# A hybrid SSD and attention layer on one core: the first head pair's softmax scaling as one GpSimd product per tile, and one weight remainder on GpSimd

## The chip, the core and the metric

The kernel runs as one program on one core of a Trainium2 chip. The core's engines are called by short names here: PE multiplies matrices (PEld is its weight load), DVE, ACT and POOL (GpSimd) are the three engines for elementwise work, and SP only issues DMAs. The metric is the device time of one execution in microseconds (us); lower is better. Each engine works through its own instructions strictly in the order in which they were issued to it, so an instruction that waits holds up everything behind it on its engine.

## The reference

One layer is computed for 512 frames of a new stream and 64 frames of a running one (256 past frames), 576 tokens in all. What matters here is the attention half, an MLA with 8 heads, and the end of the SSD half:

```
y   = y_scan + d_skip * xh
y   = y.reshape(T, 512) * silu(z)
y_ssd = rmsnorm(y, ssd_norm)                      # gate and norm of the SSD half

s   = (q_lat @ keys_c.T + q_rope @ keys_r.T) * scale
s   = where(causal, s, -inf)
w   = softmax(s)                                  # exp(s - max) / sum, per row and head
o   = (w @ keys_c) @ w_uv                         # per head

x   = x + concat([y_ssd, o]) @ w_out
x   = x + (silu(hf @ w_gate) * (hf @ w_up)) @ w_down,  hf = rmsnorm(x)
```

## The kernel before, in words

Activations lie with channels on the 128 partitions and the 576 tokens along the free axis. A product in near full precision is made of three passes: each weight tile and each operand is split into a high part (rounded on ACT) and a low part, the remainder (on DVE, one subtraction); `split_weights` (lines 107 to 113) does it for weights. The remainders of the weights of the four head pairs are called `wl_pair`, those of the output product `wl_out`.

The heads are handled in four pairs p = 0 to 3. `pair_proj(p)` (L610) loads and splits a pair's weights, and issues four DMAs on POOL's queue (L616) that copy the rotary rows of the queries into `qs`, of which there are two buffers, used by turns. `scores(p, i)` (L665) makes the score products of a query tile i: tiles 0 to 3 hold 128 new-stream queries each and see 128, 256, 384 or 512 keys per head; tile 4 holds the running stream's 64 queries of both heads, stacked on the partitions, and sees 320 keys. `soft` (L648) then does the softmax: per head a row maximum on DVE (L655) and an exponential on ACT (L656) that also sums each row into `sm`, one reciprocal of the sums on DVE (L657), and the scaling of each head's probabilities `pr` by its inverse sum, head 0 on DVE (L662) and head 1 on ACT (L660). `turn` and `turn_s` (L684, L698) transpose the probabilities on PE (`ptp`) for the value product.

Between these stand the steps of the SSD half's end. `norm_y` makes the factor `Ry` in two halves of 288 tokens: L173 `nr_v` and L178 `nr_u` and L179 `Ry` on DVE, three activations on ACT. `cat_tile(t)` scales one of four channel tiles by `Ry` on DVE (L764, `xsd`), rounds it on ACT (L143) and takes the remainder on DVE (L145, both parts are called `cat_y`). `out_tile` for F0 is the first product that uses `cat_y` (PE, `ps_o`, L458); its sums are added to x on DVE (L750).

The order of the program's steps is written by hand as strings of step names:

```
ORDER_ATT = "q11 N S03 y0 y1 y2 S01 S02 S00 S04 S13 y3 T00 X t0 S12 S11 T02 T01 F0 S14 p2 q20 V0 k20 k21 q21 S23 ..."
```

S03 is `scores(0, 3)`, N `norm_y`, y0 to y3 `cat_tile`, T and t the transposes, F0 the first output tile, p2 and p3 `pair_proj`. The order in which each engine issues its instructions is then fixed by a second set of tables, one list of places per engine (`ISSUE`), in which pieces of later steps go ahead of earlier ones; `issue_in_order` ties each instruction of an engine to the one before it.

Of the kernel before, what the change touches and what calls it, by code (L numbers as in the profile page):

```python
# [1350 lines left out]
173 189 182 184 190-191 179 192-194 185-186 220 195 204-206 196-202 207 282 208 212-214 209 216 218 215 210 221 217 219  # L1351
222-225 228 226-227 229-230 239 249 240 231 288 250 241 233 242 251 253 252 254 234 232 258 235 255 236 257 256 301 261
237 259 238 260 243 262 264 245 263 247 244 268 246 248 269-270 283 265 284 271-273 289 280 274 276 275 281 266 291 311
285 277 312 267 292 296 293 310 294 278-279 313 297 300 286-287 290 303 306 298 320 299 304 302 307 321 356 305 322 316
295 317 308 357 324 318 314 323 309 330 315 319 358 327 361 331 325-326 359 334 332 328-329 335 338 343 333 344 339 336
340 346 345 337 349 352 360 341 353 351 342 354 350 347 355 362 371 348 364-365 363 366 369-370 367-368 376 384 372 378
377 379-380 373 383 381 374 391 382 375 387 399 389 385 390 388 386 394 393 395 392 397 396 414 400 398 402 401 403 406
404 411 408 405 407 412 456 410 415 417 413 458 419 416 418 409 427 425 420 426 423 422 421 432 424 428 463 457 430 429
431 433 436 435 437 460 434 438 445 459 440 461-462 446-447 439 441 449 448 442 467 469 450 471 470 468 451 466 464 472
452-453 443-444 473 454 475 474 455 465 476 485 481 477 490-491 478 482 492-493 483 494-496 479-480 497 504 484 509-512  # L1360
516 486 498 513 500 514 501 515 502 526-529 533 540 487-489 530 541-543 499 505-506 503 517 531 523-524 518-519 507-508
525 532 534 522 544 535 560 520 536 521 545 537 539 546 538 561-562 547-548 563 549 568 564 550-553 555 569-570 554 559
571 556 572-575 565 576-577 566 557 584-585 578 586 579-580 558 592 567 593-594 587-588 581-582 595 583 597 596 589
598-601 590 604 591 602-603 614-617 605 621 606 618 607-608 619-620 613 628-630 622 631 611 632 612 623 610 609 624 635
633 625 634 627 626 648-650 636 651 637 656 652 638-641 643 657-658 642 647 659 644 660-663 653 664-665 654 645 672-673
666 674 667-668 646 680 655 681-682 675-676 669-670 683 671 685 684 677 686-689 678 692 679 690-691 702-705 693 709 694
706 695-696 707-708 701 716-718 710 719 699 720 700 711 698 697 712 723 721 713 722 715 714 736-738 724 739 725 744 740
726-729 731 745-746 730 735 747 732 748-751 741 752-753 742 733 760-761 754 762 755-756 734 768 743 769-770 763-764
757-758 771 759 773 772 765 774-777 766 780 767 778-779 790-793 781 797 782 794 783-784 795-796 789 804-806 798 807 787
# [8 lines left out]
136 127 137 134 128 140 135 124 121 120 139 129 138 141 130 123 143 131 125 150 146 149 132 210 133 145 148 154 152 151  # L1378
147 158-159 157 144 155 160-162 153 164-165 212 170 172 171 166 168 180 186 169 181 174 187 175 173 176 189 167 190 177
227 178 192 179 193 188 182 195 194 191 183 200 196 184-185 199 201 197 213 208 215-216 202-203 219 209 204 217 234 218  # L1380
198 205-206 211 214 226 220 233 221 240 207 223 242 224 222 241 229 243-244 225 271 235 230 228 231 238 237 272 232 245
236 248 239 246 249-252 247 257 255 261 254 262 256 259 263 258 278 265 253 267 266 264 268-270 260 273-277 284 280-282
285 287 283 279 293 286 291 288 290 289 302 292 294 296 295 298 300 297 301 303-304 299 309 305-306 310 307 312 329 308
311 316-317 313-315 330 318 331 319-320 332 336 321-325 333 337 335 334 326 338 340 339 327 346 343 328 344 355-356
341-342 347-348 357 349 358 350 363 352 351 353 345 354 372 359 373 360-361 374-375 382-383 364-370 384 371 376 362 381
385 380 386 377 379 378 390-392 388 387 389 393 401 394 402 395 400 397 399 396 409 398 410 403 418-419 405-408 411 420
413 421 414-415 412 416-417 404 422 427 424 428 423 425-426 435-436 429 444-445 431-433 430 434 437 446 438 447 440-441
439 442-443 448 456-457 449 458 450 454 451 455 453 452 459 464 460 465-466 462 461 463 467 475 468 476 469 474 471 473
470 483 472 484 477 492-493 479-482 485 494 487 495 488-489 486 490-491 478 496 501 498 502 497 499-500 509-510 503
518-519 505-507 504 508 511 520 512 521 514-515 513 516-517 522 530-531 523 532 524 528 525 529 527 526 533 538 534  # L1390
539-540 536 535 537 541 549 542 550 543 548 545 547 544 557 546 558 551 566-567 553-556 559 568 561 569 562-563 560
564-565 552 570 575 572 576 571 573-574 583-584 577 592-593 579-581 578 582 585 594 586 595 588-589 587 590-591 596
604-605 597 606 598 602 599 603 601 600 607 612 608 613-614 610 609 611 615 623 616 624 617 622 619 621 618 632 620 633
625 641-642 628-631 634 643 636 644 637-638 635 639-640 626 645 650 627 651 647-648 646 649 659-660 652 668-669 655-657
653 658 661 670 663 671 664-665 662 666-667 672 677-678 654 679 675 673-674 676 680-682 684 683 685-687
# [110 lines left out]
```

## Time and profile before

| | before |
|---|---|
| time, median of 3 runs | 635.08 us (634.49 to 635.43) |
| the profiled execution's own time | 634.74 us |
| its span | 633.0 us |
| mean granted TensorE clock | 0.998 |
| busy: PE, DVE, ACT, POOL | 98%, 85%, 63%, 19% |

The span is the stretch from the first to the last instruction in the trace; the 1.7 us more of the execution's own time lie around it. Busy shares are those of the whole span. The place that the change touches is a stretch of some 20 us about a quarter of the way in, from 143 to 163 us, where the SSD half ends and the attention begins.

### The profile page before, as it was taken

What the parts mean: (1) busy time and instruction counts of PE and PEld (TensorE: products, weight loads), DVE (VectorE), ACT (ScalarE), POOL (GpSimd) and SP (SyncE); (2) the same over time, 40 slices, a digit from 0 to 9 for tenths busy, and PEclk for the clock granted to TensorE, in tenths of its full rate; (3) what the DMA queues carried; (4) which work ended last, traced back from release to release, by engine and by line L of the source; (5) the groups of instructions that cost most, each with busy time, mean ns of one, the idle gap of its engine ahead of it and who ended that gap; (6) DMA issues with size and microseconds to landing.
All of it is one profiled execution on the core that took longest, in us unless ns stands there. A gap on an engine that the chain in (4) does not pass through costs nothing.

```text
span 633.0 us, 12094 instructions
## 1 busy us (share of the span) xinstructions
PE 622.7 (98%) x4635; PEld 596.3 (94%) x4635; DVE 539.3 (85%) x939; ACT 400.4 (63%) x768; POOL 117.7 (19%) x170
## 2 busy tenths in 40 slices
PE   9999999999999999999999999999999999999995
PEld 9899999986787899999999999999999999999995
DVE  6999986789776699999999888988899789976555
ACT  7655346779775567666556676566657665767364
POOL 1322104231010000001301330033104220323323
PEclk9999999999999999999999999999999999999999
DMA  8322374413231223335743986397738893689924
GB/s 320 134 61 74 95 193 127 128 61 106 77 117 34 96 72 126 89 106 178 262 128 90 221 182 152 82 193 185 169 100 162 199 202 101 100 215 251 256 41 149
DMA packets 39593, 89.19 MB, mean 141 GB/s; under 512 B 4570, under 2 KB 14312, under 8 KB 39280
## 3 DMA queue, kind: packets, MB, share of 16 engines
q1 hardware_dynamic: 26416, 63.12, 31.0%
q0 software_dynamic: 12400, 24.73, 21.3%
q8 instruction: 36, 0.59, 0.4%
q10 hardware_dynamic: 720, 0.57, 0.3%
q14 instruction: 21, 0.17, 0.1%
HBM read 62.74 MB, written 24.53 MB: 138 GB/s over the span
## 4 chain that ended last, share of the span: by engine, by line
PE 88%; DVE 6%; ACT 2%; issue 2%; POOL 1%; DMA 1%; POOLq 0%; DVEq 0%
PE ps_x L874 21%; PE ps_d L1064 14%; PE ps_z L874 10%; PE ps_in L281 7%; PE ps_y L874 5%; PE ps_o L458 4%; PE ps_z L458 4%; PE ps_first L129 3%; PE ps_d L281 2%; PE sc L672 2%; PE ps_p L874 2%; PE ps_l L281 2%; PE pv L719 1%; PE ptp L694 1%; PE ps_q L458 1%
## 5 line engine op out<-in xcount | busy, mean ns | idle before, releaser
L874 PE MATMUL ps_x<-xop,wh_gu_S 128*128 128x288 f32 x378 | 76.9, 295 | 0.0
L112 DVE TENSOR_TENSOR wl_gu_S<-gu,wh_gu_S 128x1024 fp32r<-128x1024 f32 x44 | 53.3, 1220 | 9.1 <-ACT wh_gu_S L111 6.2
L874 PEld LDWEIGHTS ps_x<-xop,wh_gu_S 128*128 128x128 f32 x378 | 60.5, 188 | 0.0
L1078 POOL DMA_DIRECT2D acc<-fz x32 | 27.9, 902 | 166.5 <-ACT fz L1075 137.8
L111 ACT CAST wh_gu_S<-gu 128x1024 fp32r<-128x1024 f32 x44 | 46.3, 1053 | 16.3 <-PE ps_y L874 8.3
L874 PE MATMUL ps_x<-xop,wl_gu_S 128*128 128x288 f32 x189 | 55.8, 295 | 0.0
L281 PE MATMUL ps_in<-xs,wh_in 128*128 128x256 f32 (+1 forms) x256 | 51.2, 296 | 0.4 <-DVE sp_a L361 0.4
L281 PEld LDWEIGHTS ps_in<-xs,wh_in 128*128 128x128 f32 x256 | 40.8, 188 | 1.2 <-issue 1.1
L281 PE MATMUL ps_in<-xs,wl_in 128*128 128x320 f32 (+1 forms) x128 | 37.7, 295 | 0.0
L874 PEld LDWEIGHTS ps_x<-xop,wl_gu_S 128*128 128x128 f32 x189 | 35.6, 188 | 0.0
L111 ACT CAST wh_gu_A<-gu 128x1024 fp32r<-128x1024 f32 x22 | 23.1, 1050 | 10.6 <-PE ps_x L874 7.2
L874 PE MATMUL ps_z<-xop,gu_a 128*128 128x288 f32 x189 | 29.5, 294 | 0.0
L458 PE MATMUL ps_o<-cat_y,wh_out 128*128 128x256 f32 (+1 forms) x128 | 28.9, 311 | 0.5 <-DVE cat_y L145 0.3
L112 DVE TENSOR_TENSOR wl_gu_A<-gu,wh_gu_A 128x1024 fp32r<-128x1024 f32 x22 | 26.8, 1218 | 1.5 <-ACT wh_gu_A L111 1.3
L1023 POOL DMA_DIRECT2D acc<-dn x8 | 4.4, 544 | 121.5 <-ACT dn L1022 121.5
L874 PE MATMUL ps_x<-xop_last,wh_gu_S 128*128 128x288 f32 x126 | 26.9, 295 | 0.0
L874 PEld LDWEIGHTS ps_z<-xop,gu_a 128*128 128x128 f32 x189 | 26.5, 188 | 0.0
L1064 PE MATMUL ps_d<-pair,d_1h 128*128 128x288 f32 x128 | 26.4, 296 | 0.0
L874 PE MATMUL ps_z<-xop,wh_gu_S 128*128 128x288 f32 x126 | 26.0, 295 | 0.0
L458 PE MATMUL ps_z<-xs,wh_z 128*128 128x256 f32 (+1 forms) x128 | 25.8, 296 | 0.1
L874 PE MATMUL ps_y<-xop,wh_gu_A 128*128 128x288 f32 x126 | 25.8, 296 | 0.0
L458 PE MATMUL ps_o<-cat_o,wh_out 128*128 128x320 f32 (+1 forms) x128 | 25.4, 294 | 0.3 <-DVE x L750 0.3
(418 smaller groups left out, 2164.1 us busy)
## 6 DMA issues: line engine op xcount, KB each, us to landing
gu<-in_w_gu SPq DMA_DIRECT2D x44, 512.0 KB, 5.3
wr_d<-in_w_down SPq DMA_DIRECT2D x18, 512.0 KB, 4.2
acc<-fz POOLq DMA_DIRECT2D x16, 288.0 KB, 7.2
acc<-da POOLq DMA_DIRECT2D x16, 288.0 KB, 8.0
acc<-dc POOLq DMA_DIRECT2D x16, 288.0 KB, 8.5
wr_in<-in_w_in SPq DMA_DIRECT2D x8, 512.0 KB, 3.8
wr_out<-in_w_out SPq DMA_DIRECT2D x8, 512.0 KB, 3.4
cumb<-cumD SPq DMA_DIRECT2D x5, 512.0 KB, 4.0
```

Source lines behind the costliest of these rows:

```text
L111: act.copy(hi, raw)
L112: dve.tensor_tensor(lo, raw, hi.bitcast(F32), ALU.subtract)
L129: pe.matmul(ps[:m, hf, : cols.stop - cols.start], w, x[:, cols], start=start and k == 0 and i == 0, stop=stop and k == last and i == 2,)
L281: pe.matmul(ps, w, x[:, cols], start=first and k == 0 and i == 0, stop=last and k == len(terms) - 1 and i == 2,)
L458: pe.matmul(ps[:, :n], w, x[:, cols], start=k == 0 and i == 0, stop=k == len(terms) - 1 and i == 2,)
L672: pe.matmul(s[:, :nk], qs[:, j, q0 : q0 + P], ks[:, j, :nk], start=True, stop=True)
L694: pe.transpose(pp[:, k : k + P], prs[p, i][:, j, b * P : b * P + P], ident)
L719: pe.matmul(pv[64 * j : 64 * j + 64, b * P :], V[b][:, h * HD : (h + 1) * HD], pts[p, b, j], start=b == 0, stop=True, skip_group_check=b > 0,)
L874: pe.matmul(ps, p, q, start=not onto and first and kp == kps[0] and j == 0, stop=onto or (last and kp == kps[-1] and j == 2), skip_group_c ...
L1023: pool.dma_start(acc[1][t], dn)
L1064: pe.matmul(ps, p, v, start=not onto and n == 0 and j == 0, stop=onto or (n == len(ks) - 1 and j == 2), skip_group_check=onto,)
L1078: pool.dma_start(out, src, accum_op=ALU.add)
```

## The change

For the first pair (p = 0) the nine scalings of `soft` (two for tiles 0 to 3, one for tile 4) are replaced: in place of one instruction per head on DVE and ACT, each of the five tiles gets one product on POOL over both its heads, with the inverse sums repeated along the keys. And the weight remainder of the third pair (p = 2) is subtracted on POOL in place of DVE. The other pairs keep their code. `pr` of a tile is one buffer of 128 partitions x heads x keys, so the five POOL products have 1024, 512, 768, 256 and 320 elements per partition (tiles 3, 1, 2, 0 and 4, in the order in which they come).

```diff
-    def split_weights(raw, name, wp=None):
+    def split_weights(raw, name, wp=None, sub=dve):
...
         act.copy(hi, raw)
-        dve.tensor_tensor(lo, raw, hi.bitcast(F32), ALU.subtract)
+        sub.tensor_tensor(lo, raw, hi.bitcast(F32), ALU.subtract)
         return hi, lo
...
-    def weights(src, n, name):
+    def weights(src, n, name, sub=dve):
...
-        return split_weights(raw[:, :n], name)
+        return split_weights(raw[:, :n], name, sub=sub)
...
     def pair_proj(p):
-        w = weights(a["w_pair"][p], 384, f"pair{p}")
+        w = weights(a["w_pair"][p], 384, f"pair{p}", sub=pool if p == 2 else dve)
...
         dve.reciprocal(sm[:, :n], sm[:, :n])
-        for j in range(n):
+        for j in range(n if p else 0):
             if j:
                 act.activation(pr[:, j], pr[:, j], AF.Identity, scale=sm[:, j : j + 1])
             else:
                 dve.tensor_scalar(pr[:, j], pr[:, j], sm[:, j : j + 1], None, ALU.mult)
+        if p == 0:
+            pool.tensor_tensor(pr, pr, sm[:, :n].unsqueeze(2).to_broadcast([P, n, nk]), ALU.mult)
         prs[p, i] = pr
```

The rest of the diff rewrites the `ISSUE` tables. On PE and SP the order stays what it was, and on DVE and ACT the same rows stand in the same order without those that were removed. On POOL six rows are new. This is the piece of the difference at that place of POOL's order, rows with a + are the new ones, names end in a running number, `h` is the SSD state, and `x4` is a row four times over:

```order
 L569 TENSOR_TENSOR h_2_1844<-h_1_1651,el2_1600 128x512
 L569 TENSOR_TENSOR h_3_1870<-h_2_1844,el3_1718 128x512
+L112 TENSOR_TENSOR wl_pair2_2153<-wr_pair2_2150,wh_pair2_2152 128x384
+L664 TENSOR_TENSOR pr_0_3_1946<-pr_0_3_1946,sm_1945 128x1024
+L664 TENSOR_TENSOR pr_0_1_1971<-pr_0_1_1971,sm_1970 128x512
+L664 TENSOR_TENSOR pr_0_2_1984<-pr_0_2_1984,sm_1983 128x768
+L664 TENSOR_TENSOR pr_0_0_1997<-pr_0_0_1997,sm_1996 128x256
+L664 TENSOR_TENSOR pr_0_4_2009<-pr_0_4_2009,sm_2008 128x320
 L616 DMA qs0_381<-rrp_1160 16x576 x4
 L616 DMA qs1_383<-rrp_1160 16x576 x4
```

The six new rows stand between the last `h` and the four DMAs of the third pair (`qs0`), which now come behind them. On DVE, this is the stretch before, from the scaling of the first pair's tile 2 to that of its tile 4; `wl_pair` is the remainder of the fourth pair, `mx` a row maximum, and `Ry` the norm's second half:

```order
L662 TENSOR_SCALAR pr_2_1986<-pr_2_1986,sm 128x384
L112 TENSOR_TENSOR wl_pair_2246<-wr_pair_2243,wh_pair_2245 128x384
L655 TENSOR_REDUCE mx<-sc_s 128x1
L178 TENSOR_TENSOR nr_u<-nr_u,nr_v 128x288
L657 RECIPROCAL sm<-sm 128x2
L179 SCALAR_TENSOR_TENSOR Ry<-nr_u,nr_y 128x288
L662 TENSOR_SCALAR pr_0_2000<-pr_0_2000,sm 128x128
L764 SCALAR_TENSOR_TENSOR xsd<-xsd,par,Ry 128x576
L657 RECIPROCAL sm<-sm 128x1
L655 TENSOR_REDUCE mx<-sc_3_0_2018 128x1
L764 SCALAR_TENSOR_TENSOR xsd<-xsd,par,Ry 128x576
L662 TENSOR_SCALAR pr_4_2013<-pr_4_2013,sm 128x320
```

And now the same stretch (the file has grown by two lines, so L764 is L766):

```order
L112 TENSOR_TENSOR wl_pair_2242<-wr_pair_2239,wh_pair_2241 128x384
L655 TENSOR_REDUCE mx<-sc_s 128x1
L178 TENSOR_TENSOR nr_u<-nr_u,nr_v 128x288
L657 RECIPROCAL sm<-sm 128x2
L179 SCALAR_TENSOR_TENSOR Ry<-nr_u,nr_y 128x288
L766 SCALAR_TENSOR_TENSOR xsd<-xsd,par,Ry 128x576
L657 RECIPROCAL sm<-sm 128x1
L655 TENSOR_REDUCE mx<-sc_3_0_2014 128x1
L766 SCALAR_TENSOR_TENSOR xsd<-xsd,par,Ry 128x576 x2
```

The three scalings are gone, and nothing else has moved; the reciprocals that POOL's products wait for stand where they stood.

## Rows read from the trace of the kernel before

**Rows 1.** The page, part 1: busy time (share of the span), instructions.
```profile
PE 622.7 (98%) x4635; PEld 596.3 (94%) x4635; DVE 539.3 (85%) x939; ACT 400.4 (63%) x768; POOL 117.7 (19%) x170
```

**Rows 2.** Waits of PE, whole run: us in total, times, longest us.
```profile
PE ps_o L458 <- DVE cat_y L145: 0.3, 1, 0.3
PE ps_o L458 <- DVE x L750: 0.3, 1, 0.3
```

**Rows 3.** Chain that ended last, 143 to 165 us: start, us, what.
```profile
160.63 2.28 PE ps_o L458 x15
```

**Rows 4.** Timeline of DVE, 140 to 182 us: start, us, instruction.
```profile
149.04 0.15 DVE L657 RECIPROCAL sm<-sm 128x2 f32<-128x2 f32 x1
...
150.29 0.34 DVE L662 TENSOR_SCALAR pr<-pr,sm 128x256 f32<-128x256 f32 x1
...
151.02 0.45 DVE L178 TENSOR_TENSOR nr_u<-nr_u,nr_v 128x288 f32<-128x288 f32 x1
...
152.19 0.45 DVE L179 SCALAR_TENSOR_TENSOR Ry<-nr_u,nr_y 128x288 f32<-128x288 f32 x1
152.56 0.15 DVE L657 RECIPROCAL sm<-sm 128x2 f32<-128x2 f32 x1
152.63 0.29 DVE L173 TENSOR_SCALAR nr_v<-R 128x288 f32<-128x288 f32 x1
...
153.04 0.41 DVE L662 TENSOR_SCALAR pr<-pr,sm 128x384 f32<-128x384 f32 x1
153.37 0.55 DVE L112 TENSOR_TENSOR wl_pair<-wr_pair,wh_pair 128x384 fp32r<-128x384 f32 x1
...
154.72 0.46 DVE L179 SCALAR_TENSOR_TENSOR Ry<-nr_u,nr_y 128x288 f32<-128x288 f32 x1
155.09 0.28 DVE L662 TENSOR_SCALAR pr<-pr,sm 128x128 f32<-128x128 f32 x1
155.29 0.81 DVE L764 SCALAR_TENSOR_TENSOR xsd<-xsd,par,Ry 128x576 f32<-128x576 f32 x1
...
157.41 0.38 DVE L662 TENSOR_SCALAR pr<-pr,sm 128x320 f32<-128x320 f32 x1
157.70 0.81 DVE L764 SCALAR_TENSOR_TENSOR xsd<-xsd,par,Ry 128x576 f32<-128x576 f32 x1
158.43 0.75 DVE L145 TENSOR_TENSOR cat_y<-xsd,cat_y 128x576 fp32r<-128x576 f32 x1
```

**Rows 5.** Timeline of ACT, 140 to 182 us.
```profile
149.53 0.19 ACT L656 ACTIVATION_READ_ACCUMULATOR pr<-sc,mx 128x1 f32 x1
```

**Rows 6.** Groups of POOL by form: busy us, mean ns of one.
```profile
L582 POOL TENSOR_TENSOR xsd<-xsd,sz 128x512 f32<-128x512 f32 x2 | 2.6, 1279 | 3.4 <-DVE xsd L555 2.5 <-DVE xsd L547 0.9
...
L582 POOL TENSOR_TENSOR xsd<-xsd,sz 128x256 f32<-128x256 f32 x1 | 0.7, 742 | 4.7 <-DVE sz L472 4.7
```

**Rows 7.** Timeline of POOL, 100 to 182 us.
```profile
108.63 1.09 POOL L515 TENSOR_SCALAR_AFFINE_SELECT cumb<-cumb 128x1024 f32<-128x1024 f32 x1 [6.29 <-ACT el L490]
...
132.80 1.04 POOL L569 TENSOR_TENSOR h<-h,el 128x512 f32<-128x512 f32 x1
140.14 1.43 POOL L569 TENSOR_TENSOR h<-h,el 128x512 f32<-128x512 f32 x1 [6.30 <-DVE h L570]
153.06 2.02 POOL L616 DMA_DIRECT2D qs<-rrp  x4 [11.49 <-PE sc_s L678]
```

**Rows 8.** Timeline of DVE, 130 to 145 us.
```profile
133.24 1.69 DVE L112 TENSOR_TENSOR wl_out<-wr_out,wh_out 128x1024 fp32r<-128x1024 f32 x1
...
139.98 0.69 DVE L555 TENSOR_TENSOR xsd<-xsd,ecp 128x512 f32<-128x512 f32 x1
```

**Rows 9.** Instructions of line L112: ns min/median/max, first and last start.
```profile
L112 DVE TENSOR_TENSOR wl_out<-wr_out,wh_out x8: 1209/1218/1685, 133.2 to 238.2; 128x1024 fp32r<-128x1024 f32 x8
```

**Rows 10.** DMAs of line L616, whole run.
```profile
DMA to landing us min/median/max: 2.3/4.5/5.9
```

**Rows 11.** Timeline of PE, 138 to 182 us.
```profile
173.69 2.10 PE L672 MATMUL sc<-ks,qs 100*128 100x512 f32 x6
```

More of the change, by code (lines that the diff above doesn't have):

```diff
@@ L1350 @@
 156 137 146 174 157 178 159 171-172 187 169 160 158 161-162 176 203 163 175 183 180 164 167 165-166 168 211 181 177 188
[L1351 to L1369, printed above, removed]
@@ L1370 @@
-808 788 799 786 785 800 811 809 801 810 803 802 824-826 812 827 813 833 828 814-817 819 834-835 818 823 836 820 837-840
-829 841-842 830 821 849-850 843 851 844-845 822 858 831 859-860 852 832 853 846-847 861 848 863 862 854 864-867 855 870
-856 868 874 869 875-877 881 878 857 879 871 880 873 872 882-892
+173 189 182 184 190-191 179 192-194 185-186 220 195 204-206 196-202 207 277 208 212-214 209 216 218 215 210 221 217 219
+222-225 228 226-227 229-230 239 248 240 231 249 241 233 250-252 234 232 255 235 253 236 254 295 257 237 256 238 242
@@ new lines @@
+258-259 244 246 243 263 245 247 264-265 278 260 279 266-268 283 275 269 271 270 276 261 285 305 280 272 306 262 286 290
+287 304 288 273-274 307 291 294 281-282 284 297 300 292 314 293 298 296 301 315 350 299 316 310 289 311 302 351 318 312
+308 317 303 324 309 313 352 321 355 325 319-320 353 328 326 322-323 329 332 337 327 338 333 330 334 340 339 331 343 346
+354 335 347 345 336 348 344 341 349 356 365 342 358-359 357 360 363-364 361-362 370 378 366 372 371 373-374 367 377 375
+368 385 376 369 381 393 383 379 384 382 380 388 387 389 386 391 390 408 394 392 396 395 397 400 398 405 402 399 401 406
@@ new lines @@
+450 404 409 411 407 452 413 410 412 403 421 419 414 420 417 416 415 426 418 422 457 451 424 423 425 427 430 429 431 454
+428 432 439 453 434 455-456 440-441 433 435 443 442 436 461 463 444 465 464 462 445 460 458 466 446-447 437-438 467 448
+469 468 449 459 470 479 475 471 484-485 472 476 486-487 477 488-490 473-474 491 498 478 503-506 510 480 492 507 494 508
+495 509 496 520-523 527 534 481-483 524 535-537 493 499-500 497 511 525 517-518 512-513 501-502 519 526 528 516 538 529
+554 514 530 515 539 531 533 540 532 555-556 541-542 557 543 562 558 544-547 549 563-564 548 553 565 550 566-569 559
@@ new lines @@
+570-571 560 551 578-579 572 580 573-574 552 586 561 587-588 581-582 575-576 589 577 591 590 583 592-595 584 598 585
+596-597 608-611 599 615 600 612 601-602 613-614 607 622-624 616 625 605 626 606 617 604 603 618 629 627 619 628 621 620
+642-644 630 645 631 650 646 632-635 637 651-652 636 641 653 638 654-657 647 658-659 648 639 666-667 660 668 661-662 640
+674 649 675-676 669-670 663-664 677 665 679 678 671 680-683 672 686 673 684-685 696-699 687 703 688 700 689-690 701-702
+695 710-712 704 713 693 714 694 705 692 691 706 717 715 707 716 709 708 730-732 718 733 719 738 734 720-723 725 739-740
@@ new lines @@
+724 729 741 726 742-745 735 746-747 736 727 754-755 748 756 749-750 728 762 737 763-764 757-758 751-752 765 753 767 766
+759 768-771 760 774 761 772-773 784-787 775 791 776 788 777-778 789-790 783 798-800 792 801 781 802 782 793 780 779 794
+805 803 795 804 797 796 818-820 806 821 807 827 822 808-811 813 828-829 812 817 830 814 831-834 823 835-836 824 815
+843-844 837 845 838-839 816 852 825 853-854 846 826 847 840-841 855 842 857 856 848 858-861 849 864 850 862 868 863
+869-871 875 872 851 873 865 874 867 866 876-886
@@ L1377 @@
 83 100 98 80 97 89 99 102 101 96 91 126 105 93 111 109-110 156 115 95 107-108 113 122 114 112 142 117 163 106 118-119
[L1378 to L1395, printed above, removed]
+136 127 137 134 128 140 135 124 121 120 139 129 138 141 130 123 143 131 125 150 146 149 132 206 133 145 148 154 152 151
@@ new lines @@
+147 158-159 157 144 155 160-162 153 164-165 208 170 172 171 166 168 180 185 169 181 174 186 175 173 176 187 167 188 177
+223 178 189 179 190-191 182 196 192 183-184 195 197 193 209 204 211-212 198-199 215 205 200 213 230 214 194 201-202 207
+210 222 216 229 217 236 203 219 238 220 218 237 225 239-240 221 267 231 226 224 227 234 233 268 228 241 232 244 235 242
+245-248 243 253 251 257 250 258 252 255 259 254 274 261 249 263 262 260 264-266 256 269-273 280 276-278 281 283 279 275
+289 282 287 284 286 285 298 288 290 292 291 294 296 293 297 299-300 295 305 301-302 306 303 308 325 304 307 312-313
@@ new lines @@
+309-311 326 314 327 315-316 328 332 317-321 329 333 331 330 322 334 336 335 323 342 339 324 340 351-352 337-338 343-344
+353 345 354 346 359 348 347 349 341 350 368 355 369 356-357 370-371 378-379 360-366 380 367 372 358 377 381 376 382 373
+375 374 386-388 384 383 385 389 397 390 398 391 396 393 395 392 405 394 406 399 414-415 401-404 407 416 409 417 410-411
+408 412-413 400 418 423 420 424 419 421-422 431-432 425 440-441 427-429 426 430 433 442 434 443 436-437 435 438-439 444
+452-453 445 454 446 450 447 451 449 448 455 460 456 461-462 458 457 459 463 471 464 472 465 470 467 469 466 479 468 480
@@ new lines @@
+473 488-489 475-478 481 490 483 491 484-485 482 486-487 474 492 497 494 498 493 495-496 505-506 499 514-515 501-503 500
+504 507 516 508 517 510-511 509 512-513 518 526-527 519 528 520 524 521 525 523 522 529 534 530 535-536 532 531 533 537
+545 538 546 539 544 541 543 540 553 542 554 547 562-563 549-552 555 564 557 565 558-559 556 560-561 548 566 571 568 572
+567 569-570 579-580 573 588-589 575-577 574 578 581 590 582 591 584-585 583 586-587 592 600-601 593 602 594 598 595 599
+597 596 603 608 604 609-610 606 605 607 611 619 612 620 613 618 615 617 614 628 616 629 621 637-638 624-627 630 639 632
@@ L1396 @@
+640 633-634 631 635-636 622 641 646 623 647 643-644 642 645 655-656 648 664-665 651-653 649 654 657 666 659 667 660-661
+658 662-663 668 673-674 650 675 671 669-670 672 676-678 680 679 681-683
 """,
@@ L1398 @@
 0-3 7 18 28 4 8 5 9 6 10 26 11 27 12 29 13-17 20-23 19 24-25 31 30 32-42 57 59 61 63 58 60 62 64 43-48 52-54 49-51 55-56
-65-75 77 79 81 76 83 85 87 80 82 78 89 84 86 88 90-93 95 94 96 98 97 99-109 111 110 112 114 113 115-125 127 126 128 130
-129 131-141 143 142 144 146 145 147-149 151 150 152-159
+65-66 72 67-71 73-81 83 85 87 82 89 91 93 86 88 84 95 90 92 94 96-99 101 100 102 104 103 105-115 117 116 118 120 119
+121-131 133 132 134 136 135 137-147 149 148 150 152 151 153-155 157 156 158-165
 """,
```

## Prediction

> **What bounds the kernel now.** I first read the shares: PE is busy 98% of the span, DVE 85%, POOL 19% [rows 1], so time is lost or won only where PE stands still, or where its work shifts as a whole. Next the waits of PE: near the change there is one on the low part of `cat_y`, 0.3 us (a few short ones for exponentials just before it would only make this one longer if they went), and behind it, but for the last 15 us of the run, only one more, 0.3 us on an addition to x [rows 2]. So whatever delays PE at the first output product stays to the end, but for some tenths. Next the chain of waits from 143 to 165 us: it lies on DVE without a gap from 146.69 to 160.59 us and passes to PE with the output product at 160.63 [rows 3]. DVE's timeline shows the pieces of that chain: each instruction begins some 0.08 us before the end of the last, so what one costs is the distance between two starts [rows 4]. In this stretch DVE sets the end, and a DVE instruction removed is worth its distance if what is behind it is ready.
>
> **What the change removes.** Six instructions leave DVE: the remainder of the third pair's weights and five scalings. The remainder and the first scaling are worth nothing: right behind them stands the reciprocal of tile 1, which needs the row sum that ACT reads out at 149.53 for 0.19, that is until 149.72 [rows 5], and it began just then. The other four are worth their length less the overlap, or the distance to the next start: 150.29, 0.34 less 0.08 = 0.26; 153.04 to 153.37, 0.33; 155.09 to 155.29, 0.20; 157.41 to 157.70, 0.29 [rows 4]. Sum: **1.08 us off DVE's chain.** Four scalings leave ACT too; the chain here doesn't pass through ACT, so I count nothing. The work that hides them is DVE's own, and if DVE were faster, ACT would come next (a rival below).
>
> **What it adds on POOL: rates.** Three rows price a two-input product there. With two full inputs 512 elements take 1.28 us and 256 take 0.74 [rows 6]: 2.1 ns for each element, and 0.20 us fixed. With a second input that is one value repeated, as the new products have it, 512 elements took 1.04 us (the `h` at 132.80) [rows 7]: with the same fixed part 1.64 ns. I take the second for the scalings, as nearest: 1.88, 1.04, 1.46, 0.62 and 0.72 us for tiles 3, 1, 2, 0 and 4. The bounds: the plain 2.1 ns from above (2.35, 1.28, 1.82, 0.74, 0.87), and from below an operation with a single input, 1024 elements in 1.09 us [rows 7], 0.87 ns. The remainder of the third pair, 384 elements of two full inputs, lies between the plain prices, 1.0 us; POOL does it at about 143, behind the last `h`. What it might cost DVE there is covered by the two removed instructions that are worth nothing, and PE uses it only behind the output product at 160.63.
>
> The Trainium skill, "GPSIMD Engine Reference", section "Elementwise — side-by-side cycle accounting", gives 4497 ns for a product of two inputs of 2048 elements, an estimate of 2.2 ns each, and names the two inputs as the limit; it makes no exception for a repeated one. By it the sum would be that of the first rival below, +2 us; the row at 132.80 speaks against it.
>
> **What it adds on DVE: mutual blocking.** POOL and DVE get in each other's way in this trace. A subtraction of two full tiles on DVE (`wl_out`, eight times) takes 1.21 to 1.22 us, but the one at 133.24 took 1.69 [rows 8, 9]. POOL's `h` ran from 132.80 to 133.84 then [rows 7]: the subtraction ended 1.22 us after 133.71, as if it had begun only 0.13 us ahead of POOL's end. The other way round, `h` at 140.14 took 1.43 instead of 1.04 [rows 7]: DVE's two-input addition at 139.98 ended at 140.66 [rows 8], and POOL ended 1.04 us after 140.53, so it too began 0.13 us before the other's end. I read it thus: of two such instructions the first keeps the second out. On DVE it strikes those with two inputs in SBUF: `nr_u`, `Ry`, `wl_pair`, `xsd`, `cat_y`. The new products run just beside these.
>
> **The walk.** POOL's product for a tile follows the tile's reciprocal on DVE (five of them; those of tiles 3 and 2 stand in [rows 4], the one of tile 4 began at 156.02).
> - Tile 3's reciprocal stood at 149.04 [rows 4] and stays near that, since it too follows a row sum of ACT; its product runs from about 149.1 to 151.0. `nr_u`, which could begin at 150.76 (151.02 less 0.26), gets in at 150.87 and ends at 151.31. Tile 1 waits for it until 151.17 and ends at 152.2. So `Ry` begins at 152.09, not at 152.19 less 0.26 = 151.93: of the gain of 0.26, 0.16 is gone, and DVE is 0.10 early.
> - The reciprocal of tile 2 (152.56) ends at 152.61, and POOL's product runs from 152.68 to 154.14. `wl_pair` of the fourth pair is ready at 153.37 less 0.10 less 0.33 = 152.94 and begins at 154.02: 1.08 lost, DVE is 0.65 late. This is the largest term: 1.46 us of POOL stand right where a two-input instruction has its turn.
> - The reciprocal of tile 0 is the one ahead of the second `Ry`; that `Ry` gets in first, from 155.37 to 155.83 (154.72 plus 0.65), and POOL runs from 155.69 to 156.31. `xsd` is ready at 155.29 plus 0.65 less 0.20 = 155.74 and begins at 156.18: 0.44 lost, 0.89 late.
> - The reciprocal of tile 4 comes at 156.02 plus 0.89 = 156.91; tile 4 runs on POOL from 157.13 to 157.86 and costs the second `xsd` 0.16; 1.05 late.
> - The scaling of 320 is gone (0.29): the third `xsd` and `cat_y` behind it are **0.76 us late**, and so is PE's output product, which waits for them.
>
> The ledger: 0.16 + 1.08 + 0.44 + 0.16 = 1.84 lost, 1.08 gained, +0.76 us. From the profiled execution's 634.74 that makes 635.5. The median of the runs shown is 0.34 above that execution, so I predict **635.8 us**.
>
> `nr_v`, at 152.63 right behind the reciprocal of tile 2, has one input, and the walk lets POOL pass it; no pair of the kind stands in the rows. The Trainium skill, "SBUF — State Buffer", section "Who interferes with whom", says that such a DVE instruction with a scalar blocks POOL as well when it runs in a two-port mode. By that POOL would start 0.14 later, and the sum would be +0.90 instead of +0.76.
>
> **What else moves.** The four DMAs of the third pair's queries stood at 153.06 and took POOL 2.0 us [rows 7]; they now come behind tile 4, from 157.9 to 159.9. Their slowest landing in the run took 5.9 us [rows 10], so the data is there by 166, and PE's scores of that pair come at 173.69 [rows 11]: hidden, with some 8 us to spare. PE's transposes of the first pair now wait for POOL instead of DVE and ACT; POOL is done with tiles 0 to 3 by 156.3 and with tile 4 by 157.9. They all stand ahead of the output product at 160.63, where PE waits 0.3 us already and would wait 0.76 longer, so some 1.1 us of delay there would be hidden. SP's load of the fourth pair's weights is released by POOL's remainder, which comes some 4 us before DVE's did, so it can't be late.
>
> **Rivals.**
> - *POOL at the plain rate.* If a repeated input is no cheaper in these shapes, the products take 2.1 ns an element. The same walk then loses 0.84 at the first `Ry`, 1.42 at `wl_pair`, 0.56 at the first `xsd` and 0.30 at the second, 3.12 in all: +2.04, or 637.1 us. For it: two rows of the same engine. Against it: the repeated input of `h` is of the same kind. Chance 0.22.
> - *No blocking, or little* (the other side). If the slow rows at 133.24 and 140.14 had another cause, or the products read so little that they leave room, DVE keeps its 1.08 less about 0.2, since at `wl_pair` it next waits for ACT's rounding of the same weights: -0.9, or 634.2 us. It decides once the blocking costs under 1.08 us in all; with the blocking but the lower rate of 0.87 ns the walk gives about -0.3, 634.8. For it: two rows are few. Against it: both fit one and the same offset of 0.13. Chance 0.16 for both.
> - *The DMAs or the transposes become late.* The first needs 8 us more of delay than I give them, the second 1.1; a microsecond beyond that makes 636.8. Chance 0.07.
>
> **How the numbers follow.** The forecast, from 635.3 to 636.4 with the spread of the runs, has 0.55. The range from 634.0 to 637.3 takes in the plain rate and the case without blocking, each with 0.2 of the runs' spread. What a measurement of this kernel can tell from no change is about 0.2%, 1.27 us, so from 633.8 to 636.35. Faster than that would need more than the whole 1.08: 0.05. Slower comes from the plain rate, the late transposes and the upper edge of the forecast: 0.35. The same: 0.60.
>
> **What would show it right or wrong.** In the changed trace POOL's product of 1024 elements takes 1.9 us (2.35: the plain rate); `wl_pair` of the fourth pair lasts about 1.6 us instead of 0.55 or begins a microsecond late; the first `xsd` lasts some 1.2 us; PE's output product goes on at about 161.4 instead of 160.63, and the waits behind it stay as they are. If `wl_pair` keeps its 0.55 us, the blocking was misread. If PE is late by 0.8 at 161 and not at the end, a wait further on has taken it up, and the second row of the waits is where to look.

## The result, and the profile after

| | before | changed |
|---|---|---|
| median (10 runs each) | 635.06 us (634.49 to 635.87) | 636.48 us (635.50 to 637.62) |
| ratio, 95% interval | | 1.0021 (1.0011 to 1.0031) |
| the profiled execution: own time, span | 634.74, 633.0 | 635.87, 633.9 |

The changed kernel is slower by 1.4 us; a second set of 12 runs of it gave 636.73 us, ratio 1.0028 (1.0015 to 1.0041). Predicted were 635.8 us, from 634.0 to 637.3. The single runs lie further apart than before, and the profiled one is among the shorter.

POOL's timeline after the change shows the six new instructions; a row that says x2 holds two that follow each other:

```profile
142.90 1.01 POOL L112 TENSOR_TENSOR wl_pair<-wr_pair,wh_pair 128x384 fp32r<-128x384 f32 x1 [1.35 <-ACT wh_pair L111]
149.24 3.11 POOL L664 TENSOR_TENSOR pr<-pr,sm 128x1024 f32<-128x1024 f32 x2 [5.33 <-DVE nr_v L173]
152.81 1.47 POOL L664 TENSOR_TENSOR pr<-pr,sm 128x768 f32<-128x768 f32 x1 [0.47 <-DVE sm L657]
155.61 0.81 POOL L664 TENSOR_TENSOR pr<-pr,sm 128x256 f32<-128x256 f32 x1 [1.33 <-DVE sm L657]
157.19 0.72 POOL L664 TENSOR_TENSOR pr<-pr,sm 128x320 f32<-128x320 f32 x1 [0.77 <-DVE sm L657]
157.85 1.98 POOL L616 DMA_DIRECT2D qs<-rrp  x4
```

And POOL's groups by form, with the mean of one in ns after the bar:

```profile
L664 POOL TENSOR_TENSOR pr<-pr,sm 128x1024 f32<-128x1024 f32 x1 | 1.9, 1894 | 5.3 <-DVE nr_v L173 5.3
...
L664 POOL TENSOR_TENSOR pr<-pr,sm 128x768 f32<-128x768 f32 x1 | 1.5, 1466 | 0.5 <-DVE sm L657 0.5
...
L112 POOL TENSOR_TENSOR wl_pair<-wr_pair,wh_pair 128x384 fp32r<-128x384 f32 x1 | 1.0, 1013 | 1.4 <-ACT wh_pair L111 1.4
```

The products take 1.89 us (1024 elements) and 1.47 (768), where 1.88 and 1.46 were worked out: less 0.20 fixed, 1.65 ns an element. The product of 320 elements took its 0.72; those of 512 and 256 took 1.25 and 0.81 instead of 1.04 and 0.62, as they began while DVE's `nr_u` and `Ry` were running. The remainder, two full inputs, takes 1.01, or 2.1 ns. The Trainium skill, "GPSIMD Engine Reference", "Elementwise — side-by-side cycle accounting", has the 4497 ns for an addition of two inputs of 2048 elements. The estimate of 2.2 ns an element that comes from it is borne out here for two full inputs and not for a repeated one.

DVE's timeline in the stretch that answers to [rows 4]:

```profile
150.87 0.58 DVE L178 TENSOR_TENSOR nr_u<-nr_u,nr_v 128x288 f32<-128x288 f32 x1
...
152.18 0.48 DVE L179 SCALAR_TENSOR_TENSOR Ry<-nr_u,nr_y 128x288 f32<-128x288 f32 x1
...
152.66 0.28 DVE L173 TENSOR_SCALAR nr_v<-R 128x288 f32<-128x288 f32 x1
...
153.06 1.63 DVE L112 TENSOR_TENSOR wl_pair<-wr_pair,wh_pair 128x384 fp32r<-128x384 f32 x1
...
155.49 0.46 DVE L179 SCALAR_TENSOR_TENSOR Ry<-nr_u,nr_y 128x288 f32<-128x288 f32 x1
155.99 1.05 DVE L766 SCALAR_TENSOR_TENSOR xsd<-xsd,par,Ry 128x576 f32<-128x576 f32 x1
...
159.17 0.75 DVE L145 TENSOR_TENSOR cat_y<-xsd,cat_y 128x576 fp32r<-128x576 f32 x1
```

This is the row to look at: `wl_pair`, 0.55 us before, stands on DVE for 1.63 us, from 153.06 to 154.69. POOL's product of tile 2 ended at 152.81 + 1.47 = 154.28, and 0.54 us after 154.15, 0.13 ahead of that end, `wl_pair` was done. `nr_u`, `Ry` and the first `xsd` are longer by 0.13, 0.03 and 0.24. `cat_y` comes at 159.17 instead of 158.43: 0.74 late, where the walk had 0.76.

PE's waits over the whole run (us, times, longest) no longer list the one for `cat_y`, which was 0.3 us [rows 2] and should have grown:

```profile
PE sc L674 <- ACT pr L656: 1.0, 1, 1.0
...
PE ps_o L458 <- DVE x L752: 0.3, 1, 0.3
```

What took its place shows in the windows of this stretch (busy time and, as PEclk, the share of full speed that TensorE's clock was granted) and in PE's timeline:

```profile
core 0: us, PE busy (x) PEld busy (x) DVE busy (x) ACT busy (x) POOL busy (x), PEclk, DMA share, GB/s
152.00:153.60 1.60, 0.72 (x4) 0.16 (x4) 1.60 (x6) 1.51 (x6) 1.13 (x2) 1.00 0.04 10
...
154.20:155.80 1.60, 1.60 (x3) 0.62 (x2) 1.60 (x5) 0.72 (x4) 0.27 (x2) 0.52 0.08 26
155.80:157.40 1.60, 1.60 (x4) 0.71 (x3) 1.56 (x4) 0.34 (x2) 0.83 (x2) 0.50 0.98 311
```
```profile
153.68 4.33 PE L674 MATMUL sc<-ks,qs 100*128 100x512 f32 x6 [0.96 <-ACT pr L656]
```

The same two windows and the same six score products in the kernel before:

```profile
154.20:155.80 1.60, 1.45 (x4) 0.38 (x2) 1.60 (x6) 1.60 (x7) 0.86 (x2) 1.00 0.72 152
155.80:157.40 1.60, 1.52 (x7) 0.97 (x8) 1.60 (x4) 1.53 (x5) 0.00 (x0) 1.00 1.12 414
```
```profile
153.67 1.98 PE L672 MATMUL sc<-ks,qs 100*128 100x512 f32 x4 [0.90 <-ACT pr L656]
155.86 0.91 PE L672 MATMUL sc<-ks,qs 100*128 100x384 f32 x2 [0.21 <-ACT pr L656]
```

PE stood still for 0.96 us until 153.68, waiting for exponentials, as in the kernel before for 0.90; it had been busy for 0.72 us of the 1.6 before. Then from 154.2 to 157.4 its clock was at half, the lower of its two levels (1.2 of 2.4 GHz); in the kernel before it was at 1.00 there. The six score products took until 158.01; in the kernel before they began at the same time and were done at 156.77. PE was late by its own doing now and reached the output product just when `cat_y` was ready. So two causes for the same 0.74 us stand in this one trace, and the experiments have to tell them apart.

```profile
174.43 2.10 PE L674 MATMUL sc<-ks,qs 100*128 100x512 f32 x6
```

PE's scores of the third pair, at 173.69 before [rows 11], begin 0.74 us late: the delay at `cat_y` goes on unchanged, and PE did not wait for the late DMAs of POOL (157.85).

### The profile page after: what moved, and what is told of

Same layout as the page of the kernel before. It is cut to its first block, busy times and chain, and to the rows that moved or that the text cites. A ratio compares the mean times of both kernels' runs of the same rounds, so it can differ in the third digit from the quotient of the medians.

```text
span 633.9 us, 12100 instructions
## 1 busy us (share of the span) xinstructions
PE 623.7 (98%) x4635; PEld 596.4 (94%) x4635; DVE 539.5 (85%) x933; ACT 398.3 (63%) x764; POOL 124.6 (20%) x176
## 4 chain that ended last, share of the span: by engine, by line
PE 90%; DVE 5%; ACT 2%; issue 2%; POOL 1%; DMA 1%; POOLq 0%; DVEq 0%
PE ps_x L876 21%; PE ps_d L1066 14%; PE ps_z L876 10%; PE ps_in L281 7%; PE ps_y L876 5%; PE ps_o L458 4%; PE ps_z L458 4%; PE ps_first L129 3%; PE sc L674 3%; PE ps_d L281 2%; PE ps_p L876 2%; PE ps_l L281 2%; PE pv L721 1%; PE ptp L696 1%; PE ps_q L458 1%
## 5 line engine op out<-in xcount | busy, mean ns | idle before, releaser
L112 DVE TENSOR_TENSOR wl_gu_S<-gu,wh_gu_S 128x1024 fp32r<-128x1024 f32 x44 | 53.4, 1222 | 9.3 <-ACT wh_gu_S L111 6.5
L112 DVE TENSOR_TENSOR wl_gu_A<-gu,wh_gu_A 128x1024 fp32r<-128x1024 f32 x22 | 26.9, 1222 | 1.2 <-ACT wh_gu_A L111 1.0
```

The costliest lines, as they stand in the source:

```text
L112: sub.tensor_tensor(lo, raw, hi.bitcast(F32), ALU.subtract)
```

## The experiments

Theory A is the prediction's: DVE's two-input instructions are shut out while POOL reads, and that sets the time. Theory B: PE's fallen clock makes the loss, and DVE's lateness only coincides. After the second profile a theory C was added, on the load of x. The edits shown are against the changed kernel, but for dummy, which starts from the kernel before.

The table puts the profiles of all kernels on one scale. The start of a DVE instruction ahead of the change (the last-but-one `xsd` of L555, at 139.98 before) shows how much later than before an execution got going, which differs by some tenths from one to the next. That is taken off from the start of the first `cat_y` on DVE (158.43 before) and of PE's scores of the third pair (173.69 before); the two columns on the right are what remains, us late (+) or early (-).

| kernel | xsd L555 | first cat_y | scores | cat_y late | scores late |
|---|---|---|---|---|---|
| before | 139.98 | 158.43 | 173.69 | | |
| changed | 139.96 | 159.17 | 174.43 | +0.76 | +0.76 |
| changed, second profile | 140.30 | 159.52 | 175.56 | +0.77 | +1.55 |
| wl2_only | 139.92 | 158.37 | 173.64 | 0.00 | +0.01 |
| tile2_back | 139.93 | 158.38 | 173.64 | 0.00 | 0.00 |
| wl3_late | 140.04 | 158.40 | 173.91 | -0.09 | +0.16 |
| no_scale | 139.66 | 157.38 | 173.05 | -0.73 | -0.32 |
| filler | 140.41 | 159.62 | 174.88 | +0.76 | +0.76 |
| two_scalars | 140.35 | 159.04 | 175.69 | +0.24 | +1.63 |
| dummy | 140.34 | 159.89 | 175.16 | +1.10 | +1.11 |
| x_early | 140.16 | 159.38 | 174.65 | +0.77 | +0.78 |
| x_early_filler | 139.89 | 159.11 | 174.37 | +0.77 | +0.77 |
| no_scale_x_early | 139.78 | 157.49 | 172.76 | -0.74 | -0.73 |
| pair3_late | 139.85 | 158.13 | 173.63 | -0.17 | +0.07 |

The kernel before had medians of 635.10 us beside the first four runs and 635.15 us beside the others.

**Only the remainder: wl2_only.**

```diff
-        for j in range(n if p else 0):
+        for j in range(n):
...
-        if p == 0:
-            pool.tensor_tensor(pr, pr, sm[:, :n].unsqueeze(2).to_broadcast([P, n, nk]), ALU.mult)
```

> Only the third pair's weight remainder moves to POOL; all scalings stay on DVE and ACT. Theory A (blocking: DVE's two-input instructions are held out while POOL reads, and the time follows DVE's lateness at the first cat_y): nothing is gained or lost, as before, 635.1 us (634.7 to 635.5), cat_y at 158.4. Theory B (PE's clock: the stretch from 154.2 to 157.4 at a granted clock of 0.50 to 0.52, which the changed kernel shows and the kernel before does not, makes PE late by itself, and DVE's lateness is only a coincidence): no products on POOL, no change of clock, also 635.1.

Measured: 635.13 us, ratio 1.0000 (0.9991 to 1.0009). The second part of the change is worth nothing, as both theories had it.

**Tile 2 on DVE and ACT again: tile2_back.**

```diff
+        on_pool = p == 0 and i != 2
-        for j in range(n if p else 0):
+        for j in range(0 if on_pool else n):
...
-        if p == 0:
+        if on_pool:
```

> The change, but tile 2 of the first pair is scaled on DVE and ACT as before; the other four tiles and the remainder stay on POOL. Theory A: the 1.08 us at the fourth pair's wl_pair go and the scaling of 0.33 comes back; by the walk DVE is 0.10 early at wl_pair, loses 0.45 at the first xsd and 0.16 at the second, and cat_y comes 0.02 late: 635.1 us (634.7 to 635.6), wl_pair 0.55 us long. Theory B: PE's pause at 153.7 is that for ACT's exponentials and stays, so the low clock stays, and so does the time of the changed kernel: 636.3 us.

Measured: 635.49 us, ratio 1.0007 (0.9998 to 1.0015). On DVE:

```profile
153.35 0.55 DVE L112 TENSOR_TENSOR wl_pair<-wr_pair,wh_pair 128x384 fp32r<-128x384 f32 x1
...
155.19 1.05 DVE L767 SCALAR_TENSOR_TENSOR xsd<-xsd,par,Ry 128x576 f32<-128x576 f32 x1
...
158.38 0.75 DVE L145 TENSOR_TENSOR cat_y<-xsd,cat_y 128x576 fp32r<-128x576 f32 x1
```

`wl_pair` is back at 0.55 us, the first `xsd` is shut out for 0.24 still, and `cat_y` is on time, as the walk said to 0.02 us. PE paused for as long as in the changed kernel (1.0 us for exponentials), and its clock stayed up in this stretch. A holds; B as stated, that the pause brings the low clock, doesn't.

**The remainder of the fourth pair out of POOL's way: wl3_late.** In the order of issue only, L112 of the fourth pair goes behind the copy of `pts` on DVE, and on SP the load of x ahead of the one that waits for this remainder:

```
DVE: ... mx(sc0_0_0), [wl_pair3], mx(sc0_s) ... copy pts0, wl_pair3, mx(sc1_2_0) ...
SP:  ... x2_0, wr_out0_2 ...          (before: wr_out0_2, x2_0)
```

> The change, and the fourth pair's remainder wl_pair stands on DVE behind the copy of pts (at about 164.5) instead of beside POOL's tile 2; SP loads x ahead of the next output weights, whose slot this remainder frees. Theory A: the wait of 1.08 and the remainder's own 0.47 leave the chain; behind it nu_u waits for ACT's square (153.94) and POOL's end; by the walk cat_y comes 0.10 early against the kernel before and 0.85 early against the changed one: 635.0 us (634.5 to 635.5). Theory B: PE's low clock stays and makes PE late by 0.7 as in the changed kernel: 636.3 us.

Measured: 635.74 us, ratio 1.0012 (1.0003 to 1.0021): a miss for A by 0.7 us, and not B's 636.3 either. `cat_y` came 0.09 early, as the walk had it, with POOL's product where it was; but in its new place the remainder goes ahead of a row maximum, which begins at 164.74 instead of 164.31, the scores are 0.16 late, and the median lies higher still. What the rest of it is, the profile doesn't show.

**No scalings at all: no_scale.** The POOL product of the change is left out, with nothing in its place.

> The change with the first pair's scalings left out altogether (its probabilities stay unnormalised): POOL has only the remainder, DVE and ACT have neither scalings nor anything that blocks them. Theory A: DVE keeps its 1.08 us less about 0.2 for ACT, cat_y 0.9 early against the kernel before, PE limits the gain to some 0.5 to 0.9: 634.3 us (633.8 to 634.7). Theory B: PE's pause and low clock stay: 636 us.

Measured: 634.69 us, ratio 0.9994 (0.9985 to 1.0003). DVE was early by 0.73 at `cat_y`, less than the 0.9 of the walk, and half of it was gone by the scores. This is where:

```profile
162.00 0.42 DVE L750 TENSOR_TENSOR x<-ps_o,x 128x256 f32<-128x256 f32 x1 [0.54 <-DMA x<-in_xT]
```

The addition to x waited 0.54 us for the load of x. That load stood in no sum.

**The changed kernel once more: after_again.**

> The changed kernel once more, for a second profile and more times. Theory A (blocking on DVE): wl_pair 1.63 us and cat_y at 159.17 within 0.05 again, and PE's output product of 160.63 comes 0.75 late whether or not PE's clock falls ahead of it; median 636.4 us (636.0 to 636.8). Theory B (PE's clock): if the granted clock stays at 1.00 from 154 to 158 this time, the output product is less than 0.3 late and the span is that of before, 633.3.

Measured: 636.73 us, ratio 1.0028 (1.0015 to 1.0041), a profile of 635.3 us of span. The clock fell again, but PE was later than DVE's 0.77 this time. The chain of waits from 155 to 167 us:

```profile
153.40 1.64 DVE wl_pair L112
...
155.06 0.33 SPq L118
...
155.44 8.97 DMA x<-in_xT
...
164.50 0.44 DVE x L752
...
164.99 1.06 PE ps_q L458 x6
```

It reads from top to bottom: `wl_pair` ends late on DVE; it frees the slot into which SP loads the next output weights (L118); behind that load, on SP's queue, stands the load of x, which took 8.97 us here (6.7 in the kernel before and in the first profile of the changed one); the addition to x waits for it, and PE's next product for the addition. SP issues its loads in order: in all three of these profiles x went out 0.38 us behind the output weights, so what holds up the first load holds up the next. The other loads of this stretch took longer in this profile too, the output weights 4.4 us instead of 3.5 and POOL's four DMAs 6.0 instead of 3.6 (us to landing, behind the size):

```profile
x<-in_xT SPq DMA_DIRECT2D x1, 1152.0 KB, 9.0
wr_out<-in_w_out SPq DMA_DIRECT2D x1, 512.0 KB, 4.4
...
qs<-rrp POOLq DMA_DIRECT2D x4, 36.0 KB, 6.0
```

**PE kept busy: filler.**

```diff
-            for j in range(2):
+            for j in (0, 1) * (2 if p == 0 else 1):
                 pe.matmul(s[64 * j : 64 * j + 64, :nk], qs[:, j, TP:], ks[:, j, TP:], start=True, stop=True)
```

> The change, and PE makes the score product of tile 4 twice (the same product into the same bank), 0.6 us of work in its pause of 0.96 us ahead of 153.7. Theory A: nothing changes, wl_pair and cat_y as in the changed kernel (1.63 us, 159.17), 636.4 us (636.0 to 636.8). Theory B: PE no longer pauses so long, its clock stays at 1.00 from 154 to 158, and the time goes back to 635.1.

Measured: 636.06 us, ratio 1.0013 (1.0005 to 1.0022). The windows and PE's wait at the output product:

```profile
152.00:153.60 1.60, 1.37 (x10) 0.48 (x8) 1.57 (x7) 1.53 (x5) 1.13 (x2) 1.00 0.00 0
...
154.20:155.80 1.60, 1.60 (x4) 0.60 (x4) 1.60 (x3) 0.72 (x4) 0.52 (x1) 1.00 0.02 5
155.80:157.40 1.60, 1.41 (x7) 0.78 (x6) 1.56 (x4) 0.45 (x2) 0.81 (x1) 1.00 0.67 202
```
```profile
161.82 0.41 PE L458 MATMUL ps_o<-cat_y,wh_out 128*128 128x320 f32 x1 [0.31 <-DVE cat_y L145]
```

The clock stays at 1.00, and PE still is 0.76 late, waiting 0.31 for `cat_y` as before: the blocking alone makes the 0.76. That settles A against B for the first 0.76 us. The median is also 0.4 to 0.7 below the two of the changed kernel. That alone doesn't show that the fallen clock is part of the rest: the interval, 1.0005 to 1.0022, overlaps with theirs, and the single runs speak against it (below).

**One head at a time on POOL: two_scalars.**

```diff
-            pool.tensor_tensor(pr, pr, sm[:, :n].unsqueeze(2).to_broadcast([P, n, nk]), ALU.mult)
+            for j in range(n):
+                pool.tensor_scalar(pr[:, j], pr[:, j], sm[:, j : j + 1], None, ALU.mult)
```

> The change with POOL's five products of two inputs replaced by nine scalings of one head each, one input and a scalar per partition. Theory A: POOL still shuts DVE out, but for shorter pieces: by the one-input rate of 0.87 ns a piece of tile 2 takes 0.53 us, wl_pair waits some 0.3 to 0.7 instead of 1.08, and cat_y comes between 0.1 early and 0.4 late against the kernel before: 635.3 us (634.9 to 635.6). If a scalar costs POOL as much as the repeated input (1.64 ns), the pieces sum to more than the products: 636.4. Theory B: PE's pause stays, 636.3.

Measured: 636.93 us, ratio 1.0028 (1.0018 to 1.0039). POOL's groups by form:

```profile
L665 POOL TENSOR_SCALAR pr<-pr,sm 128x512 f32<-128x512 f32 x2 | 3.1, 1562 | 5.3 <-DVE sm L657 5.3
...
L665 POOL TENSOR_SCALAR pr<-pr,sm 128x384 f32<-128x384 f32 x2 | 2.5, 1252 | 0.0
...
L665 POOL TENSOR_SCALAR pr<-pr,sm 128x256 f32<-128x256 f32 x2 | 1.9, 937 | 0.0
```

A miss: the scaling by a scalar is the dearer form. From 256 to 512 elements it grows by 2.4 ns an element (what DVE held up is within it), where the product with the repeated input takes 1.65 for both heads at once. The shorter pieces did let DVE in between (`wl_pair` lasted 0.62 us, the first `cat_y` came only 0.24 late), but POOL was done with tile 4 at 160.6, and PE waited 0.9 us for it.

**The blocking by itself: dummy.** The kernel before, with one product on POOL that nobody uses:

```diff
+    idle = ap_.tile([P, 2, 384], F32, tag="idle", name="idle")
+    pool.memset(idle, 1.0)
...
+        if (p, i) == (0, 2):
+            pool.tensor_tensor(idle, idle, sm[:, :n].unsqueeze(2).to_broadcast([P, n, nk]), ALU.mult)
         prs[p, i] = pr
```

> The kernel before, untouched on DVE and ACT, with one product of 768 elements (two inputs, one of them tile 2's inverse sums) added on POOL in a buffer that nothing else uses, released by tile 2's reciprocal; its result isn't used. Theory A: POOL runs from 152.8 to 154.25 and shuts out what DVE has there: if scalings with one input are shut out too, the scaling of 384 (0.41) lasts 1.5 us and DVE is 1.09 late; if only two-input instructions are, wl_pair lasts 1.3 us and DVE is 0.76 late. cat_y 0.76 to 1.09 late, 635.9 to 636.3 us. Theory B: DVE's delay doesn't matter to PE beyond its 0.3 us wait unless the clock falls: 635.1 without a fall.

Measured: 636.24 us, ratio 1.0016 (1.0007 to 1.0025). POOL and DVE:

```profile
153.23 1.47 POOL L666 TENSOR_TENSOR idle<-idle,sm 128x768 f32<-128x768 f32 x1 [10.63 <-DVE sm L659]
```
```profile
153.00 0.29 DVE L173 TENSOR_SCALAR nr_v<-R 128x288 f32<-128x288 f32 x1
...
153.40 1.50 DVE L664 TENSOR_SCALAR pr<-pr,sm 128x384 f32<-128x384 f32 x1
154.83 0.55 DVE L112 TENSOR_TENSOR wl_pair<-wr_pair,wh_pair 128x384 fp32r<-128x384 f32 x1
```

The scaling of 384 elements, 0.41 us before [rows 4], lasts 1.50 us: 1.09 more, and `cat_y` is 1.10 late, the scores 1.11, the median 1.09. The blocking alone, with no other change on DVE or ACT, costs what the rows of before had said. It also strikes a scaling with one input, which the walk had left open. The Trainium skill, "SBUF — State Buffer", "Who interferes with whom", has this rule: a scaling in a two-port mode and a POOL instruction shut each other out for their whole length, and who comes first wins. The trace agrees where POOL came first (0.41 became 1.50); in which mode the scaling ran it doesn't tell. The other way round, that `nr_v` holds up POOL, isn't shown. In the changed kernel POOL's product of tile 2 began at 152.81, ahead of the end of `nr_v` (152.94) and 0.08 us after the reciprocal ended, and those of tiles 0 and 4, which have no such neighbour, began 0.08 after theirs; here it was 0.15 (153.08 to 153.23, with `nr_v` until 153.29), and for tile 3 it was 0.23 (149.01 to 149.24, with `nr_v` until 149.21).

The load of x was issued late here as well, as it is behind `wl_pair`:

```profile
155.78 0.44 SPq L776 DMA_DIRECT2D x<-in_xT  x1
```

That is 155.78 against 154.32, 1.10 later on the scale of the table. It took 6.7 us, and nothing came on top of the 1.09.

**x loaded first: x_early, and with PE kept busy: x_early_filler.** In SP's order of the changed kernel `x2_0` goes ahead of `wr_out0_2`; the second kernel adds the edit of filler.

> The change, and SP issues the load of the first half of x ahead of that of the next output weights. The latter waits for wl_pair of the fourth pair, which the blocking delays, and the load of x behind it landed 0.9 us late for the addition to x in the second profile of the changed kernel. Theory A (all of the loss is DVE's 0.75 us at cat_y): 636.5 as the changed kernel. Theory C (DVE's 0.75 us, and on top of it in some executions a late x): the addition to x no longer waits for a DMA, cat_y stays at 159.2, first output product 0.75 late, median 636.0 us (635.7 to 636.3) with nothing above 636.8 but for a fallen clock.

> The change with both: x loaded first, and tile 4's score product made twice in PE's pause. Theory A: 636.5. Theory C with PE's clock as a third part: with the clock at 1.00 and x in time only the blocking is left, 0.75 us: 635.85 us (635.6 to 636.1), the spread as narrow as that of the kernel before.

Measured: 635.81 us for both, ratios 1.0011 (1.0002 to 1.0020) and 1.0013 (1.0004 to 1.0022). In both, DVE and PE are late by 0.77 and nothing else; the clock stayed up in both profiles. In x_early the load began at 144.57 and took 5.5 us, so it had landed 13 us ahead of its use. The medians are 0.66 us above the kernel before: the blocking, and no more.

**The scalings for nothing, and x first: no_scale_x_early.**

> The change with the first pair's scalings left out altogether (its probabilities stay unnormalised) and x loaded first: what the scalings would be worth if they cost nothing anywhere. Theory A: as without the early load, 634.7. Theory C: without the early load the addition to x waited 0.54 us for its DMA; that wait goes: 634.3 us (634.0 to 634.6).

Measured: 634.63 us, ratio 0.9989 (0.9980 to 0.9998). The wait for x is gone and PE keeps the whole 0.73. That is the most that moving these scalings could have brought, some 0.5 to 0.7 us.

**Out of the stretch what needn't be in it: pair3_late.** The scalings stay on DVE and ACT; the third pair's remainder is on POOL, and the fourth pair's rounding and remainder stand behind the copies of `pts`; x is loaded first.

> Scalings on DVE and ACT as before, the third pair's remainder on POOL, and the fourth pair's rounding (ACT) and remainder (DVE) moved out of the stretch, behind the copies of pts at about 161 and 164; x loaded first. No product on POOL runs beside DVE's two-input work. By the walk DVE's 0.47 and ACT's 0.42 ahead of the second nu_u go, cat_y 0.47 early, PE limits the gain to 0.3 to 0.5: 634.7 us (634.4 to 635.0). If the fourth pair's late weights hold up the output weights loaded behind them, 635.3.

Measured: 635.05 us, ratio 0.9998 (0.9989 to 1.0007). `cat_y` was 0.17 early and not 0.47, and by the scores nothing was left: another miss. No version among these that computes everything beats the kernel before by what can be measured.

## Why the prediction was right, and where it fell short

- *POOL's rates*: right to 0.01 us for tiles 3, 2 and 4. The rival of the plain rate falls: it asked for 2.35 us for tile 3, 1.89 were measured.
- *The blocking, and the walk*: shown by dummy and filler. +0.76 was worked out for `cat_y`, and +0.76 to +0.77 stands in the table for the five profiles that leave DVE and POOL as the change has them. The largest part, 1.08 at `wl_pair`, came as it stood. The small ones didn't: the gain of 0.26 ahead of the first `Ry` was eaten whole (0.16 was worked out), since POOL began tile 3 at 149.24 instead of 149.1 and ended later; in return the first `xsd` lost 0.37 instead of 0.44 and the second 0.09 instead of 0.16. That these misses cancel is luck. The +0.90 for a `nr_v` that shuts POOL out isn't borne out at tile 2. tile2_back takes out the largest term, 1.08, gives back a scaling, and lands on 0.00.
- *The void savings*: shown by wl2_only, 635.13 beside 635.10.
- *The rival of no blocking*: falls. Its price, -0.9, was that of no_scale: -0.73 at `cat_y`, but -0.4 in the time.
- *What else moves*: here a step of the prediction failed, and the median is 0.7 us above 635.8. "SP's load of the fourth pair's weights is released by POOL's remainder ..., so it can't be late" looks at the wrong load. The late instruction is `wl_pair` of the fourth pair, and behind it on SP's queue stand the next output weights and the first half of x. Their delay was costed at nothing. In the second profile of the changed kernel x landed 0.9 us after DVE was ready for it, and the scores were 0.78 later than `cat_y` explains. With x loaded first, the median falls to 635.81, the prediction's number. But the delay on SP's queue is not enough by itself: dummy has one of 1.10 us and loses nothing by it. The load must also take some 1.5 us longer than its 6.7, and no run shows what makes it do so.
- *PE's clock*: no step of the prediction had it. In both profiles of the changed kernel it was at half for some 3 us; PE lost 1.2 us by it in the first, hidden behind DVE's lateness. By the single runs it isn't what holds the median up either. A fall of that length shows in the mean granted clock of a run: it was 0.996 and 0.995 in the two profiles, 0.998 in those of filler and x_early. Of the 22 runs of the changed kernel the six at 0.999 have a median of 636.8 us, and the ten at 0.996 or less one of 636.6. Only the two longest, 638.75 and 640.49, have the lowest clocks, 0.991 and 0.992.

What makes up the 0.7 us that are left stays open. The load of x is what the runs point to, and it is not proven. Loading x first brings the median down by 0.7 to 0.9, filler by 0.4 to 0.7 within the scatter, both together by no more than the first. In tile2_back, where `cat_y` was on time, the load took 8.2 us and landed at 162.5, when it was used (162.56), and the median lay 0.4 us high.

It isn't settled why the load took 6.6 to 7.3 us in some profiles and 8.2 to 9.0 in others. Before the change it landed some 1.5 us ahead of its use (154.32 and 6.7, used at 162.51), and in the first profile after it as much ahead (155.10 and 6.7, used at 163.25), so it isn't the margin that changed; the early load was not tried on the kernel before. One rival was not tested: the change moves POOL's four DMAs from 153.06, about when the load of x goes out, to 157.85, into its middle. In dummy they stay in front of it (154.64 and 155.78), and an early x is out of their way, which fits the medians. Against it, the load took 8.4 us in no_scale, with these DMAs at 152.73.

## What to carry to other kernels

An elementwise instruction moved from DVE to POOL isn't off DVE: while it runs, DVE's two-input instructions and its scalings of tiles in SBUF stand still. So it has to be put beside idle time of DVE, or beside its row maxima and copies out of PSUM (with POOL at work the maximum at 152.86 kept its 0.28 us and the copy at 151.48 its 0.46), and its length on POOL (here 1.65 ns an element) counts against what it removes. Where an instruction becomes late, follow the buffer that it frees to the load that waits for it, and to every load behind that one on its queue. And try first with the work left out altogether: here that showed some 0.5 us in the median, 0.7 in the trace, as the most that there was to win.

## What the runs showed of the hardware

- On POOL the product with a repeated second input (1.65 ns an element) is cheaper than one of two full tiles (2.1) and than the scaling by a per-partition scalar (2.4, with what DVE held up).
- The blocking between DVE and POOL goes by whole instructions, between two-input instructions both ways (`wl_pair` on DVE 1.63 us instead of 0.55, POOL's product of 256 elements 0.81 instead of 0.62). POOL also shuts out DVE's one-input scalings of tiles in SBUF (0.41 us became 1.50); whether these shut out POOL isn't shown. By its usual length, the one that waits begins up to 0.2 us ahead of the other's recorded end.
- After a pause of PE of 0.96 and 0.95 us the clock fell in the two profiles of the changed kernel, and after one of 1.38 us in two_scalars. It did not fall at this place in tile2_back, wl3_late, x_early and dummy, whose pauses were 0.96, 0.95, 0.95 and 0.90 us. The pause alone doesn't decide it.
- One and the same load of 1152 KB (x) took from 6.6 to 9.0 us to land in this stretch.
